# Inverting the delta rule's triangles by 32x32 blocks on four tiles, and the sample states' products with a head in each quarter of the columns

## The chip, the cores and the metric

The kernel runs on one core of a Trainium2 chip. The metric is the device time of one execution in microseconds, the median of several runs. Five engines work side by side: TensorE (PE, matrix products into PSUM), VectorE (DVE), ScalarE (ACT), GpSimd (POOL) and SyncE (SP, which issues most of the DMAs). Each has its own queue and works through it in order.

## What is computed

The reference is one layer of a hybrid decoder on 256 prompt tokens and 8 x 4 sample tokens, all in float32. Most of the work is projections with weights of 2048 to 8192 columns. The part that the change touches is the gated delta rule of 8 heads with 128 dimensions each. Tokens go in chunks of C = 64; for each chunk and head

```python
M = jnp.where(strict, jnp.einsum('nbhid,nbhjd->nbhij', kb, kc) * decay, 0.0)
T = lax.linalg.triangular_solve(eye + M, jnp.broadcast_to(eye, M.shape),
                                left_side=True, lower=True, unit_diagonal=True)
u = T @ (vc * bc)
w = T @ (kb * jnp.exp(gcum)[..., None])
...
v_new = u_c - w_c @ S
o = qd @ S + a_c @ v_new
S = S * jnp.exp(gl)[..., None] + jnp.einsum('bhcd,bhce->bhde', kd, v_new)
```

The prompt starts from S = 0 and has 4 chunks of 64. Each of the 8 sample sequences has its own state S0 per head (128 x 128) and one chunk of 4 tokens, so the kernel needs k @ S0 and q @ S0 for 8 sequences, 8 heads and 4 tokens.

## The kernel before

**The main stream.** All projections run as one list of weight blocks of 512 KB (4 slices of 128 rows by 256 columns, or the like). A weight block is loaded by SP into `raw`, split into a rounded high part `hi` on ScalarE (L182) and a remainder `lo` on VectorE (`split_lo`, recorded under the helper's line L140), and then multiplied: `matmuls(i)` issues 24 products (L208, L209, L211), 128x128 weights against 288 tokens, in the F32R format, which takes one pass of the array. `hi` and `lo` are made three blocks ahead of their use (`AHEAD = 3`) from rings of 4 buffers.

**The side work.** The delta rule is written as a Python generator, `gdn(G)`, one for each group of four heads (G = 0, 1). The main loop calls `next` on it once before each block's matmuls; each `yield` is the end of a step, and what a step puts on TensorE stands between two blocks' matmuls. Within one turn of the loop the order on every queue is: `split_hi(i + 3)`, the step, `split_lo(i + 3)`, then what is due from the evacuation of earlier blocks, then `matmuls(i)`. During G = 0 those evacuations include the short convolution (`conv_evac`): POOL fills a pad (L268, L269), ScalarE copies and scales (L270, L271, L273), VectorE adds three taps (L143), POOL saves the history (L276). A second generator, `sample()`, starts after the inverse and treats the sample tokens.

**The inverse.** For a group there are 16 unit triangles of 64 x 64: 4 chunks x 4 heads. They lie in tiles [128, 8, 64], two heads on the two halves of the partitions (`rows`), and 8 pairs `q` along the free dimension. `nM` is the negated strict triangle. First the inverses of all 8x8 diagonal blocks are found by a short recurrence on VectorE (`u8`) and spread into the block diagonal `U`; `Tm` is the 32x32-blockwise transpose of `U`. Then the blocks are doubled for s = 8, 16, 32: `pairs(px, nM, Tm)` forms a product for each of the 16 triangles, ScalarE copies it to `X` (L1168), the next step forms `pairs(pq, X, U)`, and a predicated copy on VectorE (L1172) takes over only the blocks that the mask of s names; VectorE then transposes `U` into `Tm` again (L1174). `pairs` (L1144) issues 16 products of 64x64 by 64x64, in f32, each on one of two tiles: rows 0 to 63 with output partitions 0 to 63, or 64 to 127 with 64 to 127. At the end the inverses are copied into `U128` (L1181), block diagonal with two heads a matrix, which the chunk loop uses as weights (L1303).

**The sample states.** `spread_kq(p)` (POOL, L1125) places k and q of two heads into zeroed columns of `kqm`, 64 columns for a sequence, of which 8 hold its k and q. `states_of(p)` (L1132) then accumulates over the 8 sequences, in f32, the 64 columns as weights against S0 of that sequence and head (128 x 128), one head in each half of the array's columns. Four ScalarE copies for each p (L1137) bring the result to `kso`, in an order with the head in the quarter of the partitions. p = 0 stands in the step of s = 8, p = 1 in that of s = 16.

Of the kernel before, what the change touches and what calls it, by code (L numbers as in the profile page):

```python
# [16 lines left out]
P = 128  # L17
# [23 lines left out]
def _constants():  # L41
    k = np.arange(P)[:, None]
    m = np.arange(P)[None, :]
    f = {}
    f["ident"] = k == m
    f["lcum"] = (k <= m) & (k // 64 == m // 64)
    f["lrem"] = (k > m) & (k // 64 == m // 64)
    f["ones"] = np.ones((P, P))
    f["hm"] = k // 64 == m // 64
    i = np.arange(64)[None, :]  # L50
    f["lc"] = (k % 64) <= i
    f["mbias"] = np.where((k % 64) <= i, 0.0, -1e30)
    f["mask8"] = (k % 64) // 8 == i // 8
    f["i8"] = k % 8 == np.arange(8)[None, :]
    f["i8u"] = k % 8 < np.arange(8)[None, :]
    f["bo8"] = k // 8 == m // 8
    ks = k - 96
    mt = m % 32
    inb = (ks >= 0) & (ks // 4 == mt // 4)
    f["lcums"] = inb & (ks <= mt)  # L60
    f["lrems"] = inb & (ks > mt)
    f["lsp"] = ks == mt
    same = k // 4 == m // 4
    f["l4"] = same & (k <= m)
    f["mbias4"] = np.where(same & (k <= m), 0.0, -1e30)
    f["mask1s"] = same & (k % 2 == 0) & (m == k + 1)
    f["sel"] = (k // 32) == (np.arange(8)[None, :] % 4)
    f["bm3"] = (ks >= 0) & (ks // 4 == np.arange(8)[None, :])
    f["bmask"] = (k % 32) // 4 == np.arange(8)[None, :]
    f["hmask"] = (k // 64) == np.arange(2)[None, :]  # L70
    f["nlow"] = -np.concatenate([k // 64 == 1, (k // 32) % 2 == 1], 1).astype(np.float32)
    offs, cols, o = {}, [], 0
    f["quart"] = (k // 4 == m // 4) * 0.25
    f["rowhi"] = np.isin(k, (0, 2, 3, 5)) * 1.0
    f["rowlo"] = np.isin(k, (1, 4)) * 1.0
    early = ("hm", "bo8", "lcum", "lrem", "lcums", "lrems", "lsp", "bm3", "hmask")
    late = ("quart", "rowhi", "rowlo")
    for n, a in [(n, a) for n, a in f.items() if n not in early + late] + [(n, f[n]) for n in early + late]:
        if n in (early[0], late[0]):
            offs["early" if n == early[0] else "late"] = o  # L80
        a = np.broadcast_to(np.asarray(a, np.float32), (P, a.shape[1]))
        offs[n] = (o, o + a.shape[1])
        o += a.shape[1]
        cols.append(a)
    fm = np.ascontiguousarray(np.concatenate(cols, 1), dtype=np.float32)
    g = {}
    j = k % 64
    for s in (8, 16, 32):
        g[s] = (j // (2 * s) == i // (2 * s)) & ((j // s) % 2 == 0) & ((i // s) % 2 == 1)
    g["s"] = same & ((k // 2) % 2 == 0) & ((m // 2) % 2 == 1)  # L90
    io, cols, o = {}, [], 0
    for n, a in g.items():
        io[n] = (o, o + a.shape[1])
        o += a.shape[1]
        cols.append(np.asarray(a, np.int32))
    im = np.ascontiguousarray(np.concatenate(cols, 1), dtype=np.int32)
    return fm, offs, im, io


CF, CF_AT, CI, CI_AT = _constants()  # L100


@with_exitstack
def hybrid_kernel(ctx: ExitStack, tc: tile.TileContext, A):
# [15 lines left out]
    def nm(s):  # L120
        counter[0] += 1
        return f"{s}{counter[0]}"

    def gtile():
        n = nm("g")
        return gp.tile([P, 512], F32, tag="g", name=n)
# [5 lines left out]
    def bmid(ap, n):  # L132
        sh = list(ap.shape)
        return ap.unsqueeze(1).to_broadcast([sh[0], n] + sh[1:])

    act, dve, pe, gps, sp = nc.scalar, nc.vector, nc.tensor, nc.gpsimd, nc.sync


    def tt(out, a, b, op):
        dve.tensor_tensor(out=out, in0=a, in1=b, op=op)  # L140
# [4 lines left out]
    MUL, ADD, SUB, MIN, MAX = ALU.mult, ALU.add, ALU.subtract, ALU.min, ALU.max  # L145
# [80 lines left out]
    def cst(n):  # L226
        a, b = CF_AT[n]
        if a >= NL:
            return ph["late"][:, a - NL:b - NL]
        return cf[:, a:b] if a < NE else cfe[:, a - NE:b - NE]  # L230

    def msk(n):
        a, b = CI_AT[n]
        return ci[:, a:b]
# [734 lines left out]
    def gdn(G):  # L969
# [3 lines left out]
        kq, kqs, vf, vfs = gd["kq", G], gd["kqs", G], gd["v", G], gd["vs", G]  # L973
        S0 = pl.tile([P, 4, 8, P], F32, tag="S0", name=nm("S0"))
# [4 lines left out]
        def T(shape, tag):  # L979
            return pl.tile(shape, F32, tag=tag, name=nm(tag))  # L980
# [4 lines left out]

        b4 = T([P, 1152], "b4")
        Es, Ts, Xs, nMs, aTs, Us, vs, vns, junk2 = (b4[:, P * u:P * u + P] for u in range(9))
        kqm = b4.rearrange("p (a x) -> p a x", a=2)
        sqr = T([P, 1024], "vmh")
        rep4 = sqr[:, 512:1024]  # L990
        junk = sqr[:, 192:320]
        wide = rep4.rearrange("p (h q t) -> p h q t", h=4, q=4)
        U128 = T([P, 8, P], "U128")
        aT = T([P, 8, P], "aT")
        gps.memset(kqm, 0.0)
        states_in(0)
        gl = T([P, 4, 2, 64], "gl")
        ss = T([P, 22], "ss")
# [3 lines left out]
        rows = (slice(0, 64), slice(64, 128))  # L1002

        for c in range(4):
            kt = gtile()
            kv = kt.rearrange("p (h c) -> p h c", h=4)
# [74 lines left out]
        for c in range(4):  # L1081
            for hh in range(4):
                par = hh % 2
                pe.matmul(kk2[c // 2][rows[par], c % 2 * 2 + hh // 2].rearrange("p a x -> p (a x)"), kq[:, hh, c, par, :],  # L1084
                          kq[:, hh, c].rearrange("p a x -> p (a x)"), start=True, stop=True)
        nM = T([P, 8, 64], "gl")
        xt = T([P, 2, 8, 64], "xt")
        X, Tm = xt[:, 0], xt[:, 1]
        U = T([P, 8, 64], "U")
        tt(nM, Ef, bc(qc(nbr), 64), MUL)  # L1090
        tt(Ef, Ef, bc(rn[:, 0:8], 64), MUL)
        for u in range(2):
            q4 = slice(4 * u, 4 * u + 4)
            for par in range(2):
                r = rows[par]
                tt(nM[r, q4], kk2[u][r, :, par], nM[r, q4], MUL)
        for u in range(2):
            q4 = slice(4 * u, 4 * u + 4)
            for par in range(2):
                r = rows[par]  # L1100
# [1 line left out]
        yield  # L1102
        yield

        Uf, Tf = U.rearrange("p q c -> p (q c)"), Tm.rearrange("p q c -> p (q c)")
        n8 = sqr[:, 0:64].rearrange("p (q j) -> p q j", q=8)
        u8 = sqr[:, 64:128].rearrange("p (q j) -> p q j", q=8)
        t8 = sqr[:, 128:192].rearrange("p (q j) -> p q j", q=8)
# [7 lines left out]
        Xf = X.rearrange("p q c -> p (q c)")  # L1116
        mx = pl.tile([P, 2, 512], F32R, tag="vml", name=nm("mx"))
        kso = T([P, 2, P], "kso")
        pk = gtile()


        def spread_kq(p):
            for par in range(2):
                for u in range(2):
                    gps.tensor_copy(kqm[:, par, 32 * u:32 * u + 544].rearrange("p (b x) -> p b x", x=68)[:, :, 0:4],  # L1125
                                    kqs[:, u, 2 * p + par])

        def states_of(p):
            o = pk[:, p * P:p * P + P]
            for b in range(8):  # L1130
                for par in range(2):
                    pe.matmul(o[rows[par]], kqm[:, par, 64 * b:64 * b + 64], S0[:, 2 * p + par, b, :],  # L1132
                              start=(b == 0), stop=(b == 7))
            for par in range(2):
                hh = 2 * p + par
                for u in range(2):
                    act.copy(kso[32 * hh:32 * hh + 32, u, :], o[64 * par + 32 * u:64 * par + 32 * u + 32, :])  # L1137


        def pairs(out, a, b):  # L1140
            for q in range(8):
                for par in range(2):
                    r = rows[par]
                    pe.matmul(out[r, q * 64:q * 64 + 64], a[r, q, :], b[r, q, :], start=True, stop=True)  # L1144

        yield
        spread_kq(0)
        act.copy(mx[:, 0], Xf)
        gps.tensor_tensor(out=mx[:, 1], in0=Xf, in1=mx[:, 0], op=SUB)
        yield  # L1150
        yield
        n88 = gtile()
        for u in range(2):
# [3 lines left out]
        for j in range(1, 8):  # L1157
            tt(t8[:, :, 0:j + 1], u8[:, :, 0:j + 1], nb[:, :, 0:j + 1, j], MUL)
            dve.tensor_reduce(out=u8[:, :, j], in_=t8[:, :, 0:j + 1], axis=mybir.AxisListType.X, op=ADD)
        tt(U.rearrange("p q (b j) -> p q b j", b=8), u8.unsqueeze(2).to_broadcast([P, 8, 8, 8]),  # L1160
           cst("mask8").rearrange("p (b j) -> p b j", b=8).unsqueeze(1).to_broadcast([P, 8, 8, 8]), MUL)
        dve.transpose(out=Tf, in_=Uf)
        for _ in range(3):
            yield
        for s in (8, 16, 32):
            px = gtile()
            pairs(px, nM, Tm)
            act.copy(X, px.rearrange("p (q c) -> p q c", c=64))  # L1168
            yield
            pq = gtile()  # L1170
            pairs(pq, X, U)
            dve.copy_predicated(U, bmid(msk(s), 8), pq.rearrange("p (q c) -> p q c", c=64))  # L1172
            if s < 32:
                dve.transpose(out=Tf, in_=Uf)  # L1174
            if s < 32:
                states_of(s // 16)
            if s < 16:
                spread_kq(1)
            yield
        for par in range(2):  # L1180
            act.copy(U128[rows[par], :, 64 * par:64 * par + 64], U[rows[par]])  # L1181
        osm = T([P, P], "osm")
        done = []

# [11 lines left out]
        def sample():  # L1196
# [41 lines left out]
            tt(vr, vtr.rearrange("p (h d) -> p h d", h=4), bc(rsc[:, 1], P), MUL)  # L1238
            v3 = pl.tile([P, 4, P], F32R, tag="U", name=nm("v3"))
            lows(v3, vr, 1)  # L1240
# [44 lines left out]
        o = T([P, 4, 2, P], "xt")  # L1285
        for c in range(4):
            blk, half = c // 2, c % 2
            if c:
                p1 = gtile().rearrange("p (h x) -> p h x", h=4)
                for hh in range(4):  # L1290
                    pe.matmul(p1[:, hh, :], kq[:, hh, c].rearrange("p s x -> p (s x)"), S[:, hh, :],  # L1291
                              start=True, stop=True)
                for hh in range(4):
                    r = rows[hh % 2]
                    stt(v[r, c, hh // 2, :], p1[r, hh, :], G_["neg"][r, c, 2 * G + hh // 2:2 * G + hh // 2 + 1],
                        v[r, c, hh // 2, :], MUL, ADD)
                for par in range(2):
                    r = rows[1 - par]
# [10 lines left out]
            for hh in range(4):  # L1309
                r = rows[hh % 2]  # L1310
                pe.matmul(p3[hh % 2][:, hh // 2, :], kdec[r, c, hh // 2, :], v[r, c, hh // 2, :],  # L1311
                          start=True, stop=True)
# [219 lines left out]
```

## Time and profile before

| | |
|---|---|
| Median of 3 runs | 1692.72 us (1692.68 to 1695.08) |
| The profiled execution | 1691.56 us, of which the span from first to last instruction is 1689.8 us |
| Granted TensorE clock | 0.997 of full speed |
| Busy: TensorE / VectorE / ScalarE / GpSimd | 99% / 60% / 43% / 8% of the span |
| `gdn(0)`, the inverse with the states | 140.6 to 168 us |
| `gdn(1)`, the inverse with the states | 323.2 to 350.4 us |

A group of instructions in the profile is named by its line, its engine, and out<-in by the program's tile names; one f32 product shows as two matmuls and two weight loads, one F32R product as one of each. Matmuls overlap, so the durations of single matmuls add up to more than the time that they take; the chain of waits, which lists what ended last piece by piece, gives the time that a group takes of TensorE's stream.

### The profile page before, as it was taken

The page shows a single profiled execution, that of the slowest core. Times are in us where ns is not written, and L with a number is a line of the kernel's source. Part 1 is how long each engine was busy: PE and PEld are TensorE (multiplying, and loading weights), DVE is VectorE, ACT ScalarE, POOL GpSimd, SP SyncE. Part 2 cuts the span into 40 slices and gives each one's busy share as a digit, 9 for nine tenths or more (in the row PEclk, how much of TensorE's full clock was granted, in tenths as well). Part 3 has the DMA queues.
Part 4 walks back from the last instruction along what each step waited for, and adds up shares of the span by engine and source line. Part 5 has one row for each costly group of instructions (what it writes and reads, how often), then busy time and mean ns, then how long its engine had stood idle before and what let it go on. Part 6 is the DMA issues. An engine that isn't in the chain of part 4 may idle for free.

```text
span 1689.8 us, 30948 instructions
## 1 busy us (share of the span) xinstructions
PE 1679.7 (99%) x12987; PEld 1663.4 (98%) x12987; DVE 1010.8 (60%) x1310; ACT 734.7 (43%) x1071; POOL 127.9 (8%) x214
## 2 busy tenths in 40 slices
PE   9999999999999999999999999999999999999998
PEld 8999999999999999999999999999999999999997
DVE  5687976757444444546778744565446554466565
ACT  5785536344433333334455433344334443344342
POOL 2232412213300000000000000000000000000000
PEclk9999999999999999999999999999999999999998
DMA  8564376435655555555565555555555555555552
GB/s 255 159 192 138 113 207 197 139 113 166 200 163 164 169 167 163 163 168 163 168 183 174 163 166 167 166 163 163 168 166 157 170 163 169 167 164 163 164 163 81
DMA packets 274313, 279.11 MB, mean 165 GB/s; under 512 B 12731, under 2 KB 269628, under 8 KB 274168
## 3 DMA queue, kind: packets, MB, share of 16 engines
q1 hardware_dynamic: 269278, 263.65, 50.0%
q0 software_dynamic: 4336, 12.89, 2.8%
q8 instruction: 102, 1.67, 0.4%
q10 hardware_dynamic: 560, 0.59, 0.1%
q14 instruction: 37, 0.30, 0.0%
HBM read 269.61 MB, written 7.48 MB: 164 GB/s over the span
## 4 chain that ended last, share of the span: by engine, by line
PE 56%; issue 43%; DMA 1%; DVE 0%; ACT 0%; POOLq 0%; ACTq 0%; POOL 0%
PE acc L208 17%; PE acc L211 17%; PE acc L209 17%; PE g L1144 1%; PE g L1132 0%; PE g L1291 0%; PE g L1311 0%; PE g L1314 0%; DVE lo L140 0%; DMA raw<-in_w_in_dram 0%; DMA xr<-in_x_prompt_dram 0%; PE g L882 0%; PE g L1263 0%; PE g L1084 0%; PE g L1303 0%
## 5 line engine op out<-in xcount | busy, mean ns | idle before, releaser
L140 DVE TENSOR_TENSOR lo<-raw,hi 128x1024 fp32r<-128x1024 f32 (+1 forms) x509 | 615.2, 1213 | 542.7 <-ACT hi L182 540.7
L182 ACT CAST hi<-raw 128x1024 fp32r<-128x1024 f32 (+2 forms) x505 | 518.8, 1031 | 743.5 <-PE acc L209 689.7
L208 PE MATMUL acc<-xh,hi 128*128 128x288 f32 x1408 | 399.5, 299 | 0.5 <-ACT w L271 0.4
L209 PE MATMUL acc<-xl,hi 128*128 128x288 f32 x1408 | 394.5, 295 | 0.0
L211 PE MATMUL acc<-xh,lo 128*128 128x288 f32 x1408 | 302.4, 295 | 0.0
L208 PE MATMUL acc<-dh,hi 128*128 128x290 f32 x1024 | 289.3, 297 | 0.0
L209 PE MATMUL acc<-dl,hi 128*128 128x290 f32 x1024 | 288.1, 295 | 0.0
L208 PE MATMUL acc<-hh,hi 128*128 128x288 f32 x1024 | 287.5, 295 | 0.0
L209 PE MATMUL acc<-hl,hi 128*128 128x288 f32 x1024 | 287.2, 295 | 0.0
L208 PEld LDWEIGHTS acc<-xh,hi 128*128 128x128 f32 x1408 | 264.6, 188 | 3.2 <-issue 0.9
L209 PEld LDWEIGHTS acc<-xl,hi 128*128 128x128 f32 x1408 | 264.5, 188 | 1.0
L211 PEld LDWEIGHTS acc<-xh,lo 128*128 128x128 f32 x1408 | 226.0, 188 | 0.4 <-DVE lo L140 0.4
L211 PE MATMUL acc<-hh,lo 128*128 128x288 f32 x1024 | 222.5, 296 | 0.0
L211 PE MATMUL acc<-dh,lo 128*128 128x290 f32 x1024 | 219.8, 296 | 0.0
L209 PEld LDWEIGHTS acc<-dl,hi 128*128 128x128 f32 x1024 | 193.5, 189 | 0.1
L208 PEld LDWEIGHTS acc<-dh,hi 128*128 128x128 f32 x1024 | 192.8, 188 | 0.1
L208 PEld LDWEIGHTS acc<-hh,hi 128*128 128x128 f32 x1024 | 192.4, 188 | 0.0
L209 PEld LDWEIGHTS acc<-hl,hi 128*128 128x128 f32 x1024 | 192.2, 188 | 0.0
L211 PEld LDWEIGHTS acc<-hh,lo 128*128 128x128 f32 x1024 | 165.1, 188 | 0.0
L211 PEld LDWEIGHTS acc<-dh,lo 128*128 128x128 f32 x1024 | 164.2, 188 | 0.0
L208 PE MATMUL acc<-mh,hi 128*128 128x288 f32 x256 | 72.1, 298 | 0.0
L209 PE MATMUL acc<-ml,hi 128*128 128x288 f32 x256 | 71.7, 294 | 0.0
(404 smaller groups left out, 1539.8 us busy)
## 6 DMA issues: line engine op xcount, KB each, us to landing
raw<-in_w_in_dram SPq DMA_DIRECT2D x175, 512.0 KB, 3.5
raw<-in_w_up_dram SPq DMA_DIRECT2D x128, 512.0 KB, 3.7
raw<-in_w_down_dram SPq DMA_DIRECT2D x128, 512.0 KB, 3.6
raw<-in_w_o_dram SPq DMA_DIRECT2D x32, 512.0 KB, 3.7
raw<-in_w_a_out_dram SPq DMA_DIRECT2D x16, 512.0 KB, 3.7
raw<-in_w_b_out_dram SPq DMA_DIRECT2D x16, 512.0 KB, 3.6
S<-in_state_gdn_dram POOLq DMA_DIRECT2D x8, 512.0 KB, 6.2
out_dram<-S POOLq DMA_DIRECT2D x8, 512.0 KB, 4.7
```

Source lines behind the costliest of these rows:

```text
L140: dve.tensor_tensor(out=out, in0=a, in1=b, op=op)
L182: act.copy(his[i][:, k:k + step], raw[i][:, k:k + step])
L208: pe.matmul(ps[:, t, 0:n], wh, xh_, start=st, stop=False)
L209: pe.matmul(ps[:, t, 0:n], wh, xl_, start=False, stop=False)
L211: pe.matmul(ps[:, t, 0:n], l[:, k, t * P:(t + 1) * P], xh_, start=False, stop=en)
L1144: pe.matmul(out[r, q * 64:q * 64 + 64], a[r, q, :], b[r, q, :], start=True, stop=True)
```

## The change

Up to s = 16 a doubling stays within a diagonal block of 32 x 32. The new kernel therefore keeps `U`, its transpose `Tc` and the product `Xc` only as the two 32x32 diagonal blocks of each triangle, in [128, 8, 32]. `pairs` issues 32 products of 32x32 by 32x32 instead of 16 of 64x64, on the four diagonal tiles of the array in turn. The masks and all copies and transposes of these steps have half the columns. The last doubling, s = 32, is written by itself: only the off-diagonal 32x32 block of each triangle is formed, by 16 products in each of its two steps, on two tiles that read the first quarter of a half and write the second (`first`, `second`), then the other way round. The finished diagonal blocks go to `U128` by four POOL copies, the off-diagonal ones by two ScalarE copies.

The sample states now take all four heads at once, one in each quarter of the array's columns, and four of the eight sequences in each call: 4 accumulating products for each head with 32 columns of weights. `spread_kq` needs two POOL copies a call instead of four, into separate halves of `kqm`, and its second call moves up by two steps. Since the head now lies in the quarter that it needs, but sequence halves in different calls, the result is brought into `kso` by one ScalarE copy for each call (`kraw`), a 32x32-blockwise transpose on VectorE (`ktok`), two POOL copies that reorder columns, and a second transpose on VectorE.

```diff
+    f["m8"] = (k % 32) // 8 == i[:, 0:32] // 8
...
-    j = k % 64
-    for s in (8, 16, 32):
+    j, i = k % 32, i[:, 0:32]
+    for s in (8, 16):
...
-        kqm = b4.rearrange("p (a x) -> p a x", a=2)
+        kqm = b4.rearrange("p (a h x) -> p a h x", a=2, h=4)
...
-        U = T([P, 8, 64], "U")
+        ut = T([P, 512], "U")
+        Uf, Tf, Xcf = ut[:, 0:256], ut[:, 256:512], Tm.rearrange("p q c -> p (q c)")[:, 0:256]
+        U, Tc, Xc = (u.rearrange("p (q c) -> p q c", q=8) for u in (Uf, Tf, Xcf))
...
+        kraw, ktok = (sqr[:, 512 + 256 * u:768 + 256 * u] for u in range(2))
...
-        def spread_kq(p):
-            for par in range(2):
-                for u in range(2):
-                    gps.tensor_copy(kqm[:, par, 32 * u:32 * u + 544].rearrange("p (b x) -> p b x", x=68)[:, :, 0:4],
-                                    kqs[:, u, 2 * p + par])
-
-        def states_of(p):
-            o = pk[:, p * P:p * P + P]
-            for b in range(8):
-                for par in range(2):
-                    pe.matmul(o[rows[par]], kqm[:, par, 64 * b:64 * b + 64], S0[:, 2 * p + par, b, :],
-                              start=(b == 0), stop=(b == 7))
-            for par in range(2):
-                hh = 2 * p + par
-                for u in range(2):
-                    act.copy(kso[32 * hh:32 * hh + 32, u, :], o[64 * par + 32 * u:64 * par + 32 * u + 32, :])
+        kqx = b4.rearrange("p (a h b x) -> p a h b x", a=2, h=4, x=36)
+
+        def spread_kq(a):
+            for u in range(2):
+                gps.tensor_copy(kqx[:, a, :, :, 16 * u:16 * u + 4], kqs[:, u, :, 4 * a:4 * a + 4, :])
+
+        def states_of(a):
+            o = pk[:, a * P:a * P + P]
+            for b in range(4):
+                for hh in range(4):
+                    pe.matmul(o[32 * hh:32 * hh + 32], kqm[:, a, hh, 32 * b:32 * b + 32], S0[:, hh, 4 * a + b, :],
+                              start=(b == 0), stop=(b == 3))
+            act.copy(kraw[:, a * P:a * P + P], o)

         def pairs(out, a, b):
             for q in range(8):
-                for par in range(2):
-                    r = rows[par]
-                    pe.matmul(out[r, q * 64:q * 64 + 64], a[r, q, :], b[r, q, :], start=True, stop=True)
+                for w in range(4):
+                    r = slice(32 * w, 32 * w + 32)
+                    pe.matmul(out[r, q * 32:q * 32 + 32], a(r, q, w), b[r, q, :], start=True, stop=True)
...
-        for s in (8, 16, 32):
+        for s in (8, 16):
             px = gtile()
-            pairs(px, nM, Tm)
-            act.copy(X, px.rearrange("p (q c) -> p q c", c=64))
+            pairs(px, lambda r, q, w: nM[r, q, 32 * (w % 2):32 * (w % 2) + 32], Tc)
+            act.copy(Xc, px[:, 0:256].rearrange("p (q c) -> p q c", q=8))
             yield
             pq = gtile()
-            pairs(pq, X, U)
-            dve.copy_predicated(U, bmid(msk(s), 8), pq.rearrange("p (q c) -> p q c", c=64))
-            if s < 32:
-                dve.transpose(out=Tf, in_=Uf)
-            if s < 32:
-                states_of(s // 16)
-            if s < 16:
-                spread_kq(1)
-            yield
-        for par in range(2):
-            act.copy(U128[rows[par], :, 64 * par:64 * par + 64], U[rows[par]])
+            pairs(pq, lambda r, q, w: Xc[r, q, :], U)
+            dve.copy_predicated(U, bmid(msk(s), 8), pq[:, 0:256].rearrange("p (q c) -> p q c", q=8))
+            dve.transpose(out=Tf, in_=Uf)
+            states_of(s // 16)
+            yield
+
+        px = gtile()
+        first, second = ([slice(64 * par + 32 * u, 64 * par + 32 * u + 32) for par in range(2)] for u in range(2))
+        for q in range(8):
+            for r, d in zip(first, second):
+                pe.matmul(px[d, q * 32:q * 32 + 32], nM[r, q, 32:64], Tc[r, q, :], start=True, stop=True)
+        for r in second:
+            act.copy(Xc[r], px[r, 0:256].rearrange("p (q c) -> p q c", q=8))
+        for w in range(4):
+            r = slice(32 * w, 32 * w + 32)
+            gps.tensor_copy(U128[r, :, r], U[r])
+        dve.transpose(out=ktok, in_=kraw)
+        kv = ktok.rearrange("p (a e u x) -> p a u e x", a=2, e=4, u=2)
+        for a in range(2):
+            gps.tensor_copy(kraw.rearrange("p (u e a x) -> p a u e x", u=2, e=4, a=2)[:, a], kv[:, a])
+        dve.transpose(out=kso.rearrange("p u e -> p (u e)"), in_=kraw)
+        yield
+        pq = gtile()
+        for q in range(8):
+            for r, d in zip(second, first):
+                pe.matmul(pq[d, q * 32:q * 32 + 32], Xc[r, q, :], U[r, q, :], start=True, stop=True)
+        for par, (d, r) in enumerate(zip(first, second)):
+            act.copy(U128[d, :, r], pq[d, 0:256].rearrange("p (q c) -> p q c", q=8))
+        yield
```

More of the change, by code (lines that the diff above doesn't have):

```diff
@@ L994, in gdn @@
         aT = T([P, 8, P], "aT")
-        gps.memset(kqm, 0.0)
+        gps.memset(b4, 0.0)
         states_in(0)
@@ L1103, in gdn @@
         yield
-        Uf, Tf = U.rearrange("p q c -> p (q c)"), Tm.rearrange("p q c -> p (q c)")
         n8 = sqr[:, 0:64].rearrange("p (q j) -> p q j", q=8)
@@ L1150, in gdn @@
         yield
+        spread_kq(1)
         yield
@@ L1159, in gdn @@
             dve.tensor_reduce(out=u8[:, :, j], in_=t8[:, :, 0:j + 1], axis=mybir.AxisListType.X, op=ADD)
-        tt(U.rearrange("p q (b j) -> p q b j", b=8), u8.unsqueeze(2).to_broadcast([P, 8, 8, 8]),
-           cst("mask8").rearrange("p (b j) -> p b j", b=8).unsqueeze(1).to_broadcast([P, 8, 8, 8]), MUL)
+        tt(U.rearrange("p q (b j) -> p q b j", b=4), u8.unsqueeze(2).to_broadcast([P, 8, 4, 8]),
+           cst("m8").rearrange("p (b j) -> p b j", b=4).unsqueeze(1).to_broadcast([P, 8, 4, 8]), MUL)
         dve.transpose(out=Tf, in_=Uf)
```

## The prediction

> **What bounds the kernel now.** I read the page first, then the chain of waits piece by piece, then the waits of TensorE, the groups by shape, the timeline of one visit, and busy time by windows.
>
> ```profile
> span 1689.8 us, 30948 instructions
> ...
> PE 1679.7 (99%) x12987; PEld 1663.4 (98%) x12987; DVE 1010.8 (60%) x1310; ACT 734.7 (43%) x1071; POOL 127.9 (8%) x214
> ...
> PE 56%; issue 43%; DMA 1%; DVE 0%; ACT 0%; POOLq 0%; ACTq 0%; POOL 0%
> ```
>
> TensorE (PE) is busy for the whole span and everything that ended last is on it ("issue" is TensorE between two matmuls that overlap). So a microsecond taken from TensorE's stream is a microsecond of the span, and work on other engines counts only where TensorE comes to wait for it. The waits of TensorE, listed over the whole span, hold no line of the inverse or of the states (the largest is 1.2 us at the start), so today nothing there is late. What the touched lines take of the stream is in the chain in order of time (start, length, what, count):
>
> ```profile
> 140.69 1.08 PE g L1144 x32
> ...
> 145.14 1.08 PE g L1144 x32
> 146.22 1.90 PE g L1132 x32
> ...
> 162.31 1.08 PE g L1144 x32
> ...
> 191.01 0.89 PE g L1291 x8
> ```
>
> A call of pairs (L1144) issues 16 products and shows 32 matmuls: an f32 product is two passes. It takes 1.08 us, 12 times in the kernel. A call of states_of (L1132), 16 products as well, takes 1.90 us, 4 times. L1291 is the yardstick: the same f32 kind on the whole array, 128 moving columns, 0.89/8 = 111 ns a pass.
>
> The timeline of one visit, TensorE alone, shows what surrounds a burst:
>
> ```profile
> 140.26 0.43 PE L211 MATMUL acc<-xh,lo 128*128 128x288 f32 x2
> 140.62 1.15 PE L1144 MATMUL g<-xt,gl 64*64 64x64 f32 x32
> 141.69 0.40 PE L208 MATMUL acc<-xh,hi 128*128 128x288 f32 x1
> ```
>
> Main matmuls start every 0.13 us. The second of the L211 pair starts at 0.13 after 140.26, and the next thing would be due at 140.52; L1144 begins at 140.62. So entering costs about 0.1 us; leaving costs a similar 0.1 (the following L208 is 0.40 long instead of 0.29). That stays, since the number of visits stays: six steps a group before, six after.
>
> **How passes share the array.** If tiles did not overlap, L1132's passes (128 columns each) would cost 111 ns; they cost 1.90/32 = 59. Two tiles in the two column halves therefore run at once: 32 x 111/2 = 1.78, with 0.12 left over. L1144's passes have half the columns: 32 x 111/2/2 = 0.89, with 0.19 left over (6 ns a matmul, or 0.19 a burst; the row can't say which). I carry this rule to the new shapes: cost = passes x 111 ns x columns/128 / tiles, plus the rest.
>
> **Part by part, for one group of four heads; there are two.**
>
> Four calls of pairs at s = 8 and 16. Each goes from 32 passes of 64 columns on two tiles to 64 passes of 32 columns on four tiles: 64 x 111/4/4 = 0.44 us. The rest is 0.19 if it belongs to the burst, 0.38 if to each matmul. So 0.63 to 0.83 against 1.08. I take 0.83, because twice as many instructions pass through one stream: 4 x 0.25 = 1.0 us saved (1.8 by the other reading).
>
> The stage s = 32. It was two calls of pairs, and becomes two bursts of 16 products each on two diagonal tiles, 32 passes of 32 columns: 32 x 111/4/2 = 0.44, plus 0.19, is 0.63 each: 2 x 0.45 = 0.9 saved.
>
> The two calls of states_of. The 16 products keep their 128 columns and full depth, but take a quarter of the array's columns instead of a half: 32 x 111/4 = 0.89, plus 0.12, is 1.01 against 1.90: 2 x 0.89 = 1.78 saved. The trace shows two column tiles at once, never four; if four gave no more than two, this term is nought.
>
> Sum: 1.0 + 0.9 + 1.78 = 3.7 us a group, 7.4 us for the two (9.0 with 0.63 for a burst). The profiled execution took 1691.56 us (span 1689.8 and 1.8 around it), which would become 1684.2; the median shown is 1.2 us above it.
>
> **What I cost at nothing.** VectorE: predicated copies, transposes and the spreading of u8 shrink from 512 to 256 elements, from about 3 x 0.74 + 3 x 0.71 + 0.70 = 5.1 us a group to 2.2, and two new 256-element transposes give 0.7 back. ScalarE: eight kso copies of 0.26, three X copies of 0.59 and two of U128 at 0.62 (5.1 us) become eight copies no longer than 0.37 (3.0). Both lighter. GpSimd (POOL) gets six new copies in the last stage, and loses four of eight spreading copies, with the one wait for TensorE before the second spread (8.9 us in group 1, off the path). The four S0 heads are now all needed at the first states_of: the last load is issued at 279.3, lands within 8.1 us, and is first read at 328.7. The added mask is 32 columns of constants, loaded before 40 us.
>
> The new wait: VectorE's second kso transpose waits for two POOL copies, which stand behind four U128 copies and wait for VectorE's first transpose. A POOL copy lies between 0.2 us (128x32, L1125's shortest) and 0.8 (half of the 128x512 row of 1.55, L1149); six are 1.2 to 4.8 us. Behind the waiting transpose stands lo of the block three ahead, and on ScalarE a conv scaling (L273) that waits for POOL's pad copy. The cover:
>
> ```profile
> core 0: us, PE busy (x) PEld busy (x) DVE busy (x) ACT busy (x) POOL busy (x), PEclk, DMA share, GB/s
> 155.00:165.00 10.00, 10.00 (x140) 9.37 (x139) 3.78 (x4) 4.53 (x10) 0.40 (x3) 1.00 0.33 103
> 165.00:175.00 10.00, 10.00 (x103) 9.77 (x102) 8.67 (x8) 5.53 (x9) 6.18 (x4) 1.00 0.33 106
> ```
>
> Where the last stage begins (162 us), VectorE is idle for 6 of 10 us and POOL nearly all; lo is needed three blocks, some 9.6 us, later (a block is 24 x 0.133 = 3.2). A lag of 4.8 us fits. Nothing on TensorE reads kso itself until two steps on.
>
> **Rivals.**
>
> A, slower: a weight load and matmul can't be passed faster than now, whichever tile it goes to. 33.75 ns (1.08/32) is the closest spacing of any group in the chain, so no row shows a faster stream. At that price a new pairs call is 64 x 33.75 = 2.16 (+1.08, four times), states_of 1.08 (-0.82, twice), the last stage unchanged: +2.7 a group, +5.4 us, 1698.1. It decides from about 26 ns a matmul on, where the extra passes eat what states_of gives. Against it: going from 64 to 128 columns adds (1.90 - 1.08)/32 = 26 ns a pass, close to the 27.8 that the columns alone ask for on two tiles, so the present time is nearly all columns. And two matmuls do start side by side. In the first 20 ns of the burst,
>
> ```profile
> 140.61:140.63 0.02, 0.02 (x3) 0.02 (x2) 0.02 (x1) 0.00 (x0) 0.00 (x0) 1.00 0.00 0
> ```
>
> three matmuls are open, one of them the last main one, so two of L1144 began within 20 ns. The Trainium skill states the rule behind this rival (TensorEngine Tiling (Array Packing), Performance Considerations, Instruction Overhead): each matmul carries an overhead of some 60 cycles, and tiling should not be taken from a dimension that is already small, which is what 64 to 32 columns does. Its page TensorE: Matmul & The Clock Gate puts the least spacing at about 25 ns; an estimate by that figure is +0.5 a pairs call, -0.9 a states_of, -0.3 a last burst, together 0.5 us faster, 1692.2; the two starts within 20 ns don't agree with it as a limit on the whole array. Chance of A: 0.22, of which 0.04 near its break-even.
>
> B, the four tiles don't do what they say: no more than two run at once, because the two passes of a product follow each other and the next tile stands two passes later, or because the moving streams don't reach four tiles. Then pairs stays at 64 x 13.9 + 0.19 = 1.08, states_of at 1.90, and only the last stage gains 0.9 a group: 1.8 us, 1690.9. The trace speaks neither way beyond two tiles. 0.13.
>
> C, the new chain over ScalarE, VectorE and POOL makes TensorE late: 4.8 us in each group if nothing covers it, 9.6 - 7.4 = 2.2 slower, 1694.9. The windows speak against it. 0.05.
>
> **How the numbers follow.** The forecast has 0.60: 1692.72 - 7.4 = 1685.3. A measurement of this kernel can tell about 0.2%, 3.4 us, from no change (the three runs before lie 2.4 apart). The forecast's ends, 9.0 and 4 us saved (some of the tiles' overlap lost), are beyond that. B, C and A's part near break-even are within it, 0.22; A itself is beyond it on the other side, 0.18. Faster 0.60, same 0.22, slower 0.18. The range goes from 1683.0 (9.0 saved and some scatter) to 1695.0, which takes in B and C and leaves A's 0.18 outside.
>
> **What would show it.** Right: in the chain, the 64-matmul bursts at 0.6 to 0.85 us, the last two at about 0.63, states_of at about 1.0, and no wait of TensorE in the new stage. Bursts of 1.1 with states_of at 1.9 are B; bursts near 2.1 are A; a gap ahead of the last stage's second burst or of a main block just after it, released by VectorE or ScalarE, is C. The forecast is wrong if the time lies less than 3.4 us below before, above all if a 64-matmul burst costs over 1.08.

## The result, and the profile after

The changed kernel takes 1684.63 us, the median of 5 runs (1683.06 to 1687.64), against 1692.68 for the kernel before (1691.09 to 1695.08, 5 runs): 8.05 us less, a ratio of 0.9956 with a 95% interval of 0.9945 to 0.9967. The forecast was 1685.3, with a range of 1683.0 to 1695.0.

The page of the changed kernel (the same three lines as before):

```profile
span 1682.8 us, 31454 instructions
...
PE 1670.7 (99%) x13243; PEld 1655.6 (98%) x13243; DVE 1007.4 (60%) x1312; ACT 730.2 (43%) x1061; POOL 130.7 (8%) x218
...
PE 55%; issue 43%; DMA 1%; DVE 0%; ACT 0%; POOLq 0%; ACTq 0%; POOL 0%
```

TensorE is the bound as it was. It now does 256 matmuls more in 7.0 us less.

The chain of waits of the changed kernel in order of time (start, length, what, how many matmuls carry the chain), first group, from the product ahead of the inverse (L1085) to the one behind it (L1298). L1144 is pairs, L1135 states_of, L1182 and L1197 are the two bursts of the last doubling:

```profile
114.27 1.90 PE g L1085 x32
...
142.32 0.68 PE g L1144 x50
146.38 0.68 PE g L1144 x50
147.06 1.01 PE g L1135 x32
...
160.61 0.62 PE g L1182 x32
164.62 0.62 PE g L1197 x32
168.62 0.87 PE g L1298 x8
```

A pairs call issues 64 matmuls; 14 of them overlap others so far that the chain skips them. The two ends in the chain of the kernel before were

```profile
112.64 1.90 PE g L1084 x32
...
171.22 0.87 PE g L1279 x8
```

so this stretch was 171.22 - 112.64 = 58.58 us and is now 168.62 - 114.27 = 54.35. The second group's stretch went from 353.78 - 295.20 = 58.58 to 346.81 - 292.46 = 54.35 as well. That is 4.23 us in each group, 8.46 in all, and it is the sharpest measure of the change, since it leaves out the start of the kernel. There the two profiled executions differ: the first wait of TensorE for the input was 0.4 us before and is now

```profile
PE g L835 <- DMA xr<-in_x_prompt_dram: 2.1, 1, 2.1
```

The runs don't tie this wait to the change. In the five kernels below that differ from the changed one only in the inverse or the states, it is 1.9 us (tile by tile), 1.4 (every product twice) and 0.9 (longer chain), and not in the list for the other two. The other waits of the start differ as well, and from 7.6 to 11 us the granted clock of this execution is 0.50 (see the last heading). Together L1085 starts 1.63 us later, and so the spans differ by 7.0 only. The list of TensorE's waits still holds no line of the inverse.

The timeline of one pairs visit, TensorE alone, shows that entering and leaving cost what they did:

```profile
141.89 0.43 PE L212 MATMUL acc<-xh,lo 128*128 128x288 f32 x2
142.25 0.75 PE L1144 MATMUL g<-U,gl 32*32 32x32 f32 x64
142.93 0.40 PE L209 MATMUL acc<-xh,hi 128*128 128x288 f32 x1
```

From 142.25 to 142.93 is 0.68 us for 64 matmuls. Before, it was 1.07 for 32.

### The profile page after: what moved, and what is told of

It reads as the page before. It is cut to its first block, busy times and chain, and to the rows that moved or that the text cites. A ratio compares the mean times of both kernels' runs of the same rounds, so it can differ in the third digit from the quotient of the medians.

```text
span 1682.8 us, 31454 instructions
## 1 busy us (share of the span) xinstructions
PE 1670.7 (99%) x13243; PEld 1655.6 (98%) x13243; DVE 1007.4 (60%) x1312; ACT 730.2 (43%) x1061; POOL 130.7 (8%) x218
## 4 chain that ended last, share of the span: by engine, by line
PE 55%; issue 43%; DMA 1%; DVE 0%; ACT 0%; POOLq 0%; ACTq 0%; POOL 0%
PE acc L209 17%; PE acc L212 17%; PE acc L210 17%; DMA xr<-in_x_prompt_dram 0%; PE g L1144 0%; PE g L1310 0%; PE g L1330 0%; PE g L1333 0%; DVE lo L141 0%; PE g L883 0%; PE g L1135 0%; DMA raw<-in_w_in_dram 0%; PE g L1085 0%; PE g L1282 0%; PE g L1322 0%
```

## The experiments

The theory is that tiles share the array: a burst costs its passes times the columns that they move, divided by the number of tiles that run at once, plus a rest. The rivals are a fixed price for each matmul whichever its tile (A), no more than two tiles at once (B), and a new wait on the chain that makes kso (C). Bursts are read in the chain of waits, where nearly all of them repeat to 0.01 us; a stretch is measured as above. The time of a single run says little here, since the five runs of the changed kernel lie 4.6 us apart; where a kernel ran once, the stretch is given beside its time.

### Each half of the change alone

The states alone, on the kernel before (the new `spread_kq`, `states_of` and the chain to `kso`, put into the step of s = 32):

```diff
-                pe.matmul(o[rows[par]], kqm[:, par, 64 * b:64 * b + 64], S0[:, 2 * p + par, b, :], ...)
+                pe.matmul(o[32 * hh:32 * hh + 32], kqm[:, a, hh, 32 * b:32 * b + 32], S0[:, hh, 4 * a + b, :], ...)
```

> Only the sample states are changed (a head in each quarter of the columns, with the new chain to kso); the inverse is that of before. Tiles that share the array: four calls of states_of go from 1.90 to 1.01 us each, so 3.6 us below before, about 1689.1 against 1692.7, and the pairs bursts stay at 1.08. If only two tiles could run at once: states_of stays at 1.9 and the time is that of before. If the new chain over ScalarE, VectorE and GpSimd cost time: less than 3.6 gained, with a wait of TensorE in the trace.

It took 1688.93 us against 1691.72 on the same chip, ratio 0.9982 (0.9973 to 0.9992). Its chain, first group:

```profile
145.95 0.04 issue
145.99 1.15 PE g L1142 x32
147.14 1.01 PE g L1133 x32
```

States_of (L1133) is at 1.01 as forecast. The pairs burst in front of it came 0.25 us late in this kernel, after a ScalarE copy; the list of waits has 0.2 us for it. In the second group it is not late, and the stretch there is 56.81 us, 1.77 less than before.

The inverse alone, on the changed kernel with the old `spread_kq` and `states_of`:

```diff
-                pe.matmul(o[32 * hh:32 * hh + 32], kqm[:, a, hh, 32 * b:32 * b + 32], S0[:, hh, 4 * a + b, :], ...)
+                pe.matmul(o[rows[par]], kqm[:, par, 64 * b:64 * b + 64], S0[:, 2 * p + par, b, :], ...)
```

> Only the inverse is changed (32x32 blocks); the sample states are those of before. Tiles that share the array: eight pairs calls at 0.68 instead of 1.08 and four last bursts at 0.62 instead of 1.08, so 8 x 0.40 + 4 x 0.46 = 5.0 us below before, about 1687.7; together with the states alone the two parts add up to the whole change, 8.5 us. A price for each matmul whichever its tile (33.75 ns): slower than before by 8.6 us.

It took 1687.33 us, ratio 0.9976 (0.9965 to 0.9986). In its chain

```profile
145.38 0.68 PE g L1146 x50
146.07 1.90 PE g L1134 x32
...
161.48 0.62 PE g L1185 x32
```

the new bursts stand beside the old states_of (L1134). The second group's stretch is 56.15 us, 2.43 less than before. So the two parts add up: 1.77 and 2.43 are 4.20 against 4.23 us for the whole, and by the medians 1 - 0.9982 and 1 - 0.9976 are together 0.0042, against 0.0044. A, which had the inverse alone slower by 8.6 us, has fallen, and so has the part of B that left the states without a gain.

### The same products in another order

Tile by tile: all products of one tile, then those of the next, in both functions.

```diff
-            for q in range(8):
-                for w in range(4):
+            for w in range(4):
+                for q in range(8):
...
-            for b in range(4):
-                for hh in range(4):
+            for hh in range(4):
+                for b in range(4):
```

> The changed kernel with the same products in another order: in pairs all eight products of one tile, then the next tile; in states_of all four of one head, then the next head. Sharing needs neighbours in the order on different tiles: a pairs burst becomes 64 x 27.8 ns + 0.2 = 2.0 us instead of 0.68, a states_of 32 x 111 ns + 0.1 = 3.7 instead of 1.01; together 8 x 1.3 + 4 x 2.7 = 21 us slower than the changed kernel. If the bursts are short because small matmuls are cheap as such, or the array takes them in any order: 0.68 and 1.01 as before. If it looks far enough ahead for part of them: in between.

```profile
142.05 1.84 PE g L1144 x64
147.27 1.84 PE g L1144 x64
149.11 2.39 PE g L1135 x32
```

With the same instructions, a pairs burst went from 0.68 to 1.84 us and states_of from 1.01 to 2.39, and the one run took 1699.12 us. The stretch is 61.73 us in both groups, so the order alone costs 14.8 us in the two, not the 21 expected, mostly because states_of lost less than forecast. Small matmuls are thus not cheap as such: what makes them cheap is that neighbours in the queue go to different tiles. States_of is in between, as the last sentence of the expectation allowed: with no sharing it would be 32 x 111 ns = 3.55. A likely reading is that four products of one head are only 8 matmuls, so that part of the next head's overlaps them, while eight products (16 matmuls) in pairs leave almost nothing of that. No run tests this reading.

Two by two: tiles 0 and 1 in turn, then 2 and 3.

```diff
-            for q in range(8):
-                for w in range(4):
+            for q, w in [(q, 2 * v + u) for v in range(2) for q in range(8) for u in range(2)]:
...
-            for b in range(4):
-                for hh in range(4):
+            for b, hh in [(b, 2 * v + u) for v in range(2) for b in range(4) for u in range(2)]:
```

> The changed kernel with the same products in the order of two tiles in turn, first tiles 0 and 1, then 2 and 3, in pairs and in states_of. Sharing by neighbours: a pairs burst becomes 64 x 13.9 ns + 0.2 = 1.1 us, a states_of 32 x 55.6 ns + 0.12 = 1.9; 6.9 us slower than the changed kernel. If order doesn't matter: 0.68 and 1.01.

```profile
144.35 1.04 PE g L1144 x62
145.39 1.47 PE g L1135 x32
```

Pairs is at 1.04, against 1.1 by the rule for two tiles; states_of at 1.47 against 1.9, again better than the rule where a tile's share of the queue is short. The one run took 1686.89 us. The stretch is 56.69 us in both groups, 4.7 us in the two above the changed kernel, where 6.9 was expected. One tile, two tiles and four tiles at once give 1.84, 1.04 and 0.68 for the same 64 matmuls: B has fallen.

### Every product twice

```diff
-            for q in range(8):
+            for q in [q for _ in range(2) for q in range(8)]:
...
-            for b in range(4):
+            for b in [b for _ in range(2) for b in range(4)]:
```

> The changed kernel with every product of pairs and of states_of issued twice over, so that the results stay the same and a pairs burst has 128 matmuls, a states_of 64. What the second half adds is the pure price of a matmul: if the rest of a burst (0.68 - 0.44 = 0.24 us) belongs to the burst, pairs goes to 1.13; if it belongs to each matmul (3.7 ns), to 1.36; if the stream can't be fed beyond the first few dozen matmuls, well above 1.36, up to 64 x 29 ns = 1.9 more. States_of: 1.01 + 0.89 = 1.90.

```profile
160.68 1.22 PE g L1144 x82
161.90 1.88 PE g L1135 x64
```

The second 64 matmuls add 1.22 - 0.68 = 0.54 us, 8.4 ns each, where the sharing rule has 111/4/4 = 6.9. So the rest of a burst belongs to both: 1.5 ns to each matmul, and 0.68 - 64 x 8.4 ns = 0.14 to the burst. States_of adds 0.87, 27.2 ns a matmul (27.8 by the rule). The stream can be fed at this pace for 128 matmuls, each with its weight load. The one run took 1696.48 us. The Trainium skill (TensorE: Matmul & The Clock Gate, "Wait — 56ns, not 53.3ns?") has 25 ns as the least distance between two matmul starts however few columns; on four tiles in turn the mean distance here is 8.4 ns, so the figure isn't a limit on the array as a whole.

Two stops in this run are not explained by this; they are under the last heading.

### Half the columns

Only 16 of the 32 columns that a product moves are ever taken over by the mask. This kernel moves those alone, and ScalarE's copy and VectorE's predicated copy take only them as well.

```diff
+            cols = lambda u: u.rearrange("p (a t j) -> p t a j", t=2, j=s)[:, t]
...
-                    pe.matmul(out[r, q * 32:q * 32 + 32], a(r, q, w), b[r, q, :], start=True, stop=True)
+                    pe.matmul(cols(out[r, q * 32:q * 32 + 32]), a(r, q, w), cols(b[r, q, :]), start=True, stop=True)
```

> The changed kernel with only those 16 of the 32 columns moved through the array in each product of pairs that the mask of s uses (the rest is never read); same counts, same results. If a pass costs by its moving columns: 64 x 3.5 ns less 0.22 us a burst, 0.46, 1.8 us in all. If weight loads (still 32 columns) or the feeding of instructions hold the pace now: 0.68 as it is, and the time of the changed kernel, 1684.6.

```profile
143.82 0.66 PE g L1145 x54
144.47 1.01 PE g L1135 x32
```

A burst went from 0.68 to 0.66, not to 0.46. The moving columns no longer set the pace at this size; whether the weight loads (still 32 columns) do, or the supply of instructions, was not told apart. The time is 1683.29 us (ratio to before 0.9951, 0.9937 to 0.9964), whose interval overlaps that of the changed kernel: no version to prefer. By the trace it is worth 8 x 0.02 us, some 0.2.

### A longer chain to kso

```diff
-        for w in range(4):
+        for w in [w for _ in range(4) for w in range(4)]:
             r = slice(32 * w, 32 * w + 32)
             gps.tensor_copy(U128[r, :, r], U[r])
```

> The changed kernel with the four U128 copies on GpSimd made four times over, which puts 12 copies of about 0.74 us, 8.9 us in a group, ahead of the two copies that VectorE's second kso transpose waits for. If the chain is covered by the three blocks that lo runs ahead (9.6 us): VectorE waits some 10 us instead of 1.4, and TensorE waits little, under 2 us a group. If there is no such cover: TensorE waits most of the 8.9 us in each group, 15 us or more in all.

In the changed kernel VectorE's second kso transpose waits for POOL by

```profile
160.06 0.45 DVE L1192 STREAM_TRANSPOSE kso<-vmh 128x256 f32<-128x256 f32 x1 [1.41 <-POOL vmh L1191]
```

and here, VectorE and then TensorE in the timelines:

```profile
163.74 0.45 DVE L1192 STREAM_TRANSPOSE kso<-vmh 128x256 f32<-128x256 f32 x1 [6.91 <-POOL vmh L1191]
```

```profile
174.27 0.68 PE L1322 MATMUL g<-v,U 128*128 128x128 f32 x4 [2.63 <-DVE v L141]
```

The 12 copies took about 0.46 us each, not 0.74, so the wait grew by 5.5 us instead of 8.9. TensorE then stood for 2.63 us in the first group, more than was expected if the chain is covered (under 2). The stop began some 8 us after the transpose, at the first product of the chunk loop (L1322), which needs `v` from VectorE. In the second group VectorE's wait grew as much, and TensorE did not wait at all. The changed kernel's timeline shows a difference between the groups: in the first, VectorE works off convolution taps (L144, 5.16 us) just before `v`, in the second it stands idle for 2.24 us there. The one run took 1687.63 us. So C is real as a mechanism, and far from deciding in the changed kernel: 2.9 of the 5.5 added microseconds were still covered in the first group, and all in the second.

## Why the prediction was right, point by point

**TensorE is the bound, and each microsecond off its stream is one off the span.** Right: the two stretches give 8.46 us, the medians 8.05, and no wait of TensorE appeared in the new stage.

**The sharing rule, carried from two tiles to four.** That four tiles run side by side was right: the three orders show it. The terms, in us a group:

| Term | forecast | measured |
|---|---|---|
| pairs, s = 8 and 16: one burst | 0.83 (0.63 by the other reading) | 0.68 |
| saved by four of them | 1.0 | 1.6 |
| last doubling: one burst | 0.63 | 0.62 |
| saved by two | 0.9 | 0.9 |
| states_of: one call | 1.01 | 1.01 |
| saved by two | 1.78 | 1.78 |
| sum | 3.7 | 4.3 (stretch: 4.23) |

**The mis-sized term** is the rest of a pairs burst. The row of before could not say whether its 0.19 us belonged to the burst or to each matmul, and I took 6 ns a matmul "because twice as many instructions pass through one stream". Beside the rule's 6.9 ns for the columns, the doubled bursts show 1.5 ns a matmul and 0.14 us a burst, so the truth lay near the other reading; this is 0.15 us in each of eight bursts, 1.2 us.

**Where the rule came close by luck.** In states_of, with 128 moving columns, the columns do set the price: 27.2 ns a matmul against 27.8. In pairs they don't. The rule prices 64 passes of 32 columns on four tiles at 0.44 us and of 16 columns at 0.22, but halving the columns took 0.02 us off the burst. So the columns don't hold the pace of 8.4 ns a matmul, and that it lies near the rule's 6.9 is luck as far as the runs go. What does hold it, the weight loads or the supply of instructions, stays open.

**Rival A** fell with the inverse alone (faster, not slower) and with 8.4 ns a matmul, far under its 26 ns. The row that it leaned on, 33.75 ns as the closest spacing of any group, was two tiles' time for 64 columns and not a limit of the stream, as the comparison of 64 with 128 columns had suggested.

**Rival B** fell with the three orders: 1.84, 1.04, 0.68.

**Rival C** and the work costed at nothing: the new wait exists, 1.41 us on VectorE, at the place named. VectorE and ScalarE became lighter as said (busy 1007.4 and 730.2 us, from 1010.8 and 734.7). But the cover was read off the wrong reader. I counted the three blocks that lo runs ahead, 9.6 us; what came late first when the chain was stretched was `v` for the chunk loop, and in the first group it had only some 3 us to spare beyond the present wait. The six copies took 2.67 + 0.52 us, and started before the step's matmuls, since U was ready. The bound of 4.8 us would have added 1.6 us, about half of what was to spare.

## What to carry to other kernels

Where TensorE is the bound, as here, cut small f32 products so that neighbours in its queue go to different tiles. The order of issue decides whether tiling pays: the same instructions took 0.68 or 1.84 us, against 1.08 before. A first price for a tiled burst comes from a row that has two tiles, by passes x columns / tiles; test its rest by issuing the burst twice, and the columns by halving them. With 32 columns on four tiles, moving fewer columns bought next to nothing here (0.02 us), while each matmul cost 8.4 ns.

## What had not been expected

**TensorE can stand still inside a dense stretch with no wait shown.** The kernel with every product twice stopped once in each group, in the first in the middle of a states_of call:

```profile
146.88 1.87 PE g L1135 x61
148.75 2.03 issue
150.78 0.41 PE g L1135 x3
```

and in the second for 1.0 us in a pairs burst. The first came after 128 + 61 matmuls that ran without a main matmul between them. But the same 128 + 64 ran through without a stop later in that group and twice in the second, where the stop of 1.0 us came after 112 of a burst's 128 matmuls, so the length of the stretch alone is not the cause. The DMA engines were 62% busy during the first stop and idle during the second. The profile names nothing that it waited for, and no other kernel here has such a stop in its list of TensorE's waits; the cause stays open.

**After a stop of about 2 us the granted clock was halved for 3.4 us.** After the stop of 2.03 us the same kernel's windows show the granted clock (the column behind POOL's) at

```profile
core 0: us, PE busy (x) PEld busy (x) DVE busy (x) ACT busy (x) POOL busy (x), PEclk, DMA share, GB/s
...
152.30:155.30 3.00, 3.00 (x14) 3.00 (x14) 1.63 (x3) 0.21 (x1) 0.00 (x0) 0.50 0.17 57
```

and main matmuls started every 0.24 us instead of 0.13 until 155.4. The kernel with the long chain did the same after its 2.63 us (clock 0.50 from 175.1 to 178.4 us), which is why it lost more than it waited: 4.4 us up to the next product of the chunk loop. The same half clock, again for 3.4 us, followed the wait for the input at the start: after 2.08 us in the changed kernel (7.6 to 11 us) and after 1.89 us in the tile-by-tile order. It did not follow the stops of 1.03 and 1.38 us in the kernel with every product twice. The Trainium skill (TensorE: Matmul & The Clock Gate, Part 1) has the clock halve after an idle window of about 3.4 us; here stops of 1.89 to 2.63 us were followed by it. A single stop is not the only way there: near its end, among small matmuls, the kernel before falls to 0.50 from 1681.3 us on, with no wait above 0.4 us in the list just ahead of it.
